# Latent depthwise convolution on TensorE: four-channel block-diagonal matmuls replaced by one 32x64 tile per channel, with its inputs loaded one channel group ahead

## The chip, the cores and the metric

The kernel runs on one core of one Trainium2 chip. The metric is the device time of one execution in microseconds. Before the change the median of three runs is 1877.12 us (1874.78 to 1882.59). Shares and durations below come from one further execution, taken with the hardware profiler.

## The reference, cut to what matters

The reference is one layer of a hybrid backbone: a bidirectional Mamba-2 scan beside a Conformer convolution branch, for 256 context tokens and 2048 latent tokens of width 1024. All data are fp32. The changed part is the convolution branch of the latent tokens, which lie on a grid of 32 rows and 64 columns:

```python
h = ga * jax.nn.sigmoid(gb)                    # (1, 32, 64, 1024)
h = depthwise_conv(h, conv_w, conv_b)          # 31 taps along the 32 rows, each channel by itself
h = layer_norm(h, ln_g, ln_b)                  # over the channels of a token
return jax.nn.silu(h)
```

With 31 taps and 32 rows nearly every output row of a channel depends on every input row. For one channel the convolution is therefore a product of a 32x32 matrix, made of the taps, with the 32x64 grid.

## The kernel before, in words

The tokens are worked on in two halves. In each half the normalised input (`hh`, `hl`: a high and a low part, 128 x 512 pieces) is multiplied with 44 tiles of 128 columns of `w_in`, three passes each (L378, L379, L380 in `mm_cm`). For a tile pair (`gab_unit`, L528) the results `gb` and `ga` become the convolution's input, written to a DRAM tensor `GL[j]` for channel group `j` of 128 channels (L540). `silu_unit` (L542) makes the gates in the same way. These projections are the main stream of the second half, called `blocks`.

Beside this stream run two side streams: the scan (`pass_a`, L648: decay matrices on ScalarE, small matmuls `px`, `py`, `po`, `pst`) and `extra`, which holds the convolutions: for each pair of channel groups `lat_conv`, `ctx_conv` (31 taps on VectorE, L590), `lat_conv`. Python generators give the order: `interleave` (L849) takes one step of `blocks` and then as many side steps as their share, and `merge` (L49) mixes scan and `extra` by their numbers of steps. The framework's scheduler then moves instructions by its own simulated times, so that the order on an engine is not exactly the order of the code. All DMAs of the core are issued in order by SyncE (SP); an issue that waits holds up those behind it.

`lat_conv` (L603) handles one channel group in these steps:

- It loads the bias `cbb`, the taps `kd` (partition = 32 * channel within a group of four + row, 32 rows x 32 groups of four) and the grid `cx` (same partitions, 32 groups x 64 columns). `kd` and `cx` have one buffer each, so that the loads of a channel group wait until the one before has been worked off.
- `expand(u)` (L618) copies the taps of eight groups of four channels into a block-diagonal 128x128 matrix each, in `kbuf`, which was zeroed once (L931). That is four ScalarE copies of 32 x 256 per `u` (L622), sixteen per channel group. There are two `kbuf` buffers.
- For each `u` of four, eight matmuls (L634) multiply the grid of four channels (stationary, 128 rows x 64 columns) with the block-diagonal matrix (moving, 128 columns). Two halves of the channel group go to the two halves of the array's columns (`h`). All matmuls of one `u` fill one PSUM bank of the pool `ss`, which has five banks and is shared with the scan.
- VectorE adds the bias and writes the bank to `cvv` (L639); after the fourth, two DMAs write `cvv` to `CVL` (L644).

A matmul with fp32 operands appears in the profile as two records, each with its own weight load, and one with operands split beforehand (fp32r: L378 to L380, L1078) as one. The eight matmuls of one `u` are thus sixteen records; the eight channel groups make 512 records in 32 groups.

After the blocks and side streams comes the output projection (L1078) with the scan's backward pass and the layer norm that reads `CVL`.

Of the kernel before, what the change touches and what calls it, by code (L numbers as in the profile page):

```python
# [8 lines left out]
F32 = mybir.dt.float32  # L9
# [4 lines left out]
MUL, ADD, SUB, MAX, MIN = ALU.mult, ALU.add, ALU.subtract, ALU.max, ALU.min  # L14
# [3 lines left out]
P = 128  # L18
# [49 lines left out]
def backbone_kernel(ctx, tc, xa, xt_in, cols, rows, wconv, conf_b, gp_row, bg_row, state0, w_mod, w_dt, w_in, w_out,  # L68
                    y_ctx, y_lat, new_state):
    nc = tc.nc  # L70
    V, S, G, T, DMA = nc.vector, nc.scalar, nc.gpsimd, nc.tensor, nc.sync
# [5 lines left out]
    def bank(tag, name):  # L77
        return psp.tile([P, 512], F32, tag=tag, name=name, bufs=3 if tag == "mm" else 5)

    def dram(name, shape):  # L80
        return drp.tile(shape, F32, tag=name, name=name)
# [4 lines left out]
    GL = [dram(f"gl{j}", [P, NT * P]) for j in range(KT)]  # L86
# [87 lines left out]
    cp = ph_c.enter_context(tc.tile_pool(name="cp", bufs=1, side="right"))  # L174

    def ev(name):
        return evp.tile([P, 512], F32, tag="ev", name=name, bufs=3)
# [162 lines left out]
    def load_w(half, c0):  # L340
        t = WCOL.index(c0)
        wl = wp.tile([P, KT, P], F32R, tag="wl", name=f"wl{c0}_{half}", bufs=3)
        wh = wp.tile([P, KT, P], F32R, tag="wh", name=f"wh{c0}_{half}", bufs=3)
        flat = lambda w: w.bitcast(F32).rearrange("p k n -> p (k n)")
        if half:
            DMA.dma_start(flat(wh), WHD[t])
            DMA.dma_start(flat(wl), WLD[t])
            return wh, wl
        for u in range(2):
            ks = slice(4 * u, 4 * u + 4)  # L350
            wr = wp.tile([P, 4, P], F32, tag="wr", name=f"wr{c0}_{u}", bufs=2)
            DMA.dma_start(wr.rearrange("p k n -> p (k n)"), w_in[t * P:(t + 1) * P, u * 512:(u + 1) * 512])
            S.copy(wh[:, ks, :], wr)  # L353
            V.tensor_tensor(wl[:, ks, :], wr, wh[:, ks, :].bitcast(F32), SUB)
        DMA.dma_start(WHD[t], flat(wh))
        DMA.dma_start(WLD[t], flat(wl))
        return wh, wl
# [10 lines left out]
    def next_w():  # L368
        while len(wq) < 3 and wcols:
            wq.append(load_w(*wcols.pop(0)))  # L370
        return wq.pop(0)

    def mm_cm(ps, w, h):
        wh, wl = w
        hh, hl = h
        BN = hh.shape[2]
        for k in range(KT):
            T.matmul(ps[:, :BN], wh[:, k, :], hh[:, k, :], start=(k == 0), stop=False)  # L378
            T.matmul(ps[:, :BN], wh[:, k, :], hl[:, k, :], start=False, stop=False)  # L379
            T.matmul(ps[:, :BN], wl[:, k, :], hh[:, k, :], start=False, stop=(k == KT - 1))  # L380
            yield
# [101 lines left out]
    def xbc_phase(half, first, hb, prep, tails, dtp):  # L483
# [41 lines left out]
        for _ in dtp:  # L525
            pass

    def gab_unit(half, j, hb):  # L528
        wb = next_w()
        wa = next_w()  # L530
        for b in ORDER[half]:
            BN, o = BNS[b], TOK[b]
            pg = bank("mm", f"gb{half}_{j}_{b}")
            yield from mm_cm(pg, wb, hb[b])
            th = ev(f"gth{half}_{j}_{b}")[:, :BN]
            S.activation(th, pg[:, :BN], AF.Tanh, scale=0.5)  # L536
            pa_ = bank("mm", f"ga{half}_{j}_{b}")
            yield from mm_cm(pa_, wa, hb[b])
            V.scalar_tensor_tensor(th, th, 1.0, pa_[:, :BN], ADD, MUL)  # L539
            DMA.dma_start(GL[j][:, o:o + BN], th)  # L540

    def silu_unit(half, c0, dst, j, hb, order=None):  # L542
        w = next_w()
        for b in order or ORDER[half]:
            BN, o = BNS[b], TOK[b] - half * HT[0] * P
            ps = bank("mm", f"sp{half}_{c0}_{j}_{b}")
            yield from mm_cm(ps, w, hb[b])
            th = ev(f"sth{half}_{c0}_{j}_{b}")[:, :BN]
            S.activation(th, ps[:, :BN], AF.Tanh, scale=0.5)  # L549
            V.scalar_tensor_tensor(th, th, 1.0, ps[:, :BN], ADD, MUL)  # L550
            DMA.dma_start(dst[half][j * P:(j + 1) * P, o:o + BN], th)
# [28 lines left out]
    def ctx_conv(j, tile):  # L580
        g = tile(f"cg{j}")
        G.memset(g[:, 0:15], 0.0)
        G.memset(g[:, 271:286], 0.0)
        DMA.dma_start(g[:, 15:271], GL[j][:, 0:256])
        yield
        acc = g[:, 512:768]
        w0 = C_CONFW + j * CW
        V.tensor_scalar(acc, g[:, 0:256], cv[:, w0:w0 + 1], cfb2[:, j:j + 1], MUL, ADD)
        for t in range(1, CW):
            V.scalar_tensor_tensor(acc, g[:, t:t + 256], cv[:, w0 + t:w0 + t + 1], acc, MUL, ADD)  # L590
            if t % 3 == 0:
                yield
        ps = bank("ss", f"cps{j}")
        for t in range(2):
            T.transpose(ps[:, t * P:(t + 1) * P], acc[:, t * P:(t + 1) * P], ident)
        o = g[:, 768:1024]
        S.mul(o, ps[:, :256], 0.5)
        DMA.dma_start(CVC[:, j * P:(j + 1) * P].rearrange("(t p) c -> p t c", p=P),
                      o.rearrange("p (t c) -> p t c", c=P))
        yield  # L600


    def lat_conv(j, lp, kbuf):  # L603
        cbb = lp.tile([P, HD], F32, tag="cbb", name=f"cbb{j}", bufs=2)
        for h in range(2):
            c0 = j * P + h * 64
            DMA.dma_start(cbb[h * 64:(h + 1) * 64], conf_b[c0:c0 + 64].partition_broadcast(64))
        kd = lp.tile([P, 32, 32], F32, tag="kd", name=f"kd{j}", bufs=1)
        for c4 in range(4):
            src = bass.AP(tensor=wconv.tensor, offset=(j * 4 + c4) * 64 * 32, ap=[[32, 32], [1, 1024]])  # L610
            DMA.dma_start(kd[c4 * 32:(c4 + 1) * 32].rearrange("p r g -> p (r g)"), src)

        x = lp.tile([P, 32, 64], F32, tag="cx", name=f"cx{j}", bufs=1)
        src = GL[j][:, 256:].rearrange("(g c) (r w) -> c r g w", c=4, w=64)
        for c4 in range(4):
            DMA.dma_start(x[c4 * 32:(c4 + 1) * 32], src[c4])

        def expand(u):  # L618
            kt = kbuf[u % 2]
            for c4 in range(4):  # L620
                rs = slice(c4 * 32, (c4 + 1) * 32)
                S.copy(kt[rs, :, rs].rearrange("p (h q) r -> p h q r", h=2),  # L622
                       kd[rs].rearrange("p r (h u q) -> p u h q r", h=2, u=4)[:, u])

        vt = lp.tile([P, 32, HD], F32, tag="cvv", name=f"cvv{j}", bufs=1)
        yield
        expand(0)
        yield
        for u in range(4):
            kt = kbuf[u % 2]  # L630
            ps = bank("ss", f"cp{j}_{u}")
            for q in range(4):
                for h in range(2):
                    T.matmul(ps[h * 64:(h + 1) * 64, q * P:(q + 1) * P], x[:, h * 16 + u * 4 + q, :], kt[:, h * 4 + q, :],  # L634
                             start=True, stop=True)
            if u < 3:
                expand(u + 1)
            yield
            V.scalar_tensor_tensor(vt[:, ::-1, u * 16:(u + 1) * 16].rearrange("p r c -> p c r"),  # L639
                                   ps.rearrange("p (c r) -> p c r", r=32), 0.5,  # L640
                                   cbb[:, u * 16:(u + 1) * 16].unsqueeze(2).to_broadcast([P, 16, 32]), MUL, ADD)
        for h in range(2):
            c0 = j * P + h * 64
            DMA.dma_start(CVL[:, c0:c0 + 64].rearrange("(r w) c -> w r c", w=64), vt[h * 64:(h + 1) * 64])  # L644
        yield


    def pass_a(i):  # L648
# [213 lines left out]
    def chain(gens):  # L862
        for g in gens:
            yield from g
# [5 lines left out]
    def post(half, nb):  # L870
        return chain([gab_unit(half, j, hb) for j in range(8)] + [silu_unit(half, Z0, ZS, j, hb) for j in range(8)]
                     + [silu_unit(half, GS0, GS, j, hb) for j in range(nb)])
# [33 lines left out]
    extra = chain([gate_rows()] + [ctx_conv(j, big) for j in range(4)])  # L906
# [19 lines left out]
    ph_b[0].close()  # L926
    ph_l = ExitStack()
    lp = ph_l.enter_context(tc.tile_pool(name="lp", bufs=1, side="right"))
    kbuf = [lp.tile([P, 8, P], F32, name=f"kbuf{u}") for u in range(2)]
    for u in range(2):  # L930
        G.memset(kbuf[u], 0.0)  # L931
    blocks = post(1, 5)
    cg = lambda name: lp.tile([P, D], F32, tag="cg", name=name, bufs=2)
    extra = chain(f for j in range(4) for f in (lat_conv(2 * j, lp, kbuf), ctx_conv(j + 4, cg), lat_conv(2 * j + 1, lp, kbuf)))
    sc_ = scan(range(9, NT))
    run(take(blocks, 24))
    interleave(take(blocks, 24), [sc_] * 4, 24)
# [292 lines left out]
```

## Time and profile before

| what | value |
|---|---|
| median of three runs | 1877.12 us (1874.78 to 1882.59) |
| profiled execution | 1882.2 us, its span 1880.5 us |
| TensorE (PE) busy | 1825.6 us, 97% |
| weight loads (PEld) busy | 1504.6 us, 80% |
| VectorE (DVE) busy | 1188.2 us, 63% |
| ScalarE (ACT) busy | 839.5 us, 45% |
| GpSimd (POOL) busy | 269.0 us, 14% |
| mean DMA rate | 200 GB/s |
| mean granted TensorE clock | 0.986 |
| latent convolution's first and last matmul | 957.8 us and 1336.9 us after the start |

How to read it: a row of the groups gives line, engine, operation, output and inputs by the program's names, sizes and count; then the busy time, the mean time of one in ns, and the idle time of the engine just before, with what ended it. In the timeline the first two columns are start and duration in us, and equal instructions that follow each other are merged into one row. In the waits the columns are the total in us, how often, and the longest. The end of a matmul is modelled, so that the step from one start to the next says more than the duration. PEclk is the share of the full TensorE clock that was granted.

### The profile page before, as it was taken

The page shows a single profiled execution, that of the slowest core. Times are in us where ns is not written, and L with a number is a line of the kernel's source. Part 1 is how long each engine was busy: PE and PEld are TensorE (multiplying, and loading weights), DVE is VectorE, ACT ScalarE, POOL GpSimd, SP SyncE. Part 2 cuts the span into 40 slices and gives each one's busy share as a digit, 9 for nine tenths or more (in the row PEclk, how much of TensorE's full clock was granted, in tenths as well). Part 3 has the DMA queues.
Part 4 walks back from the last instruction along what each step waited for, and adds up shares of the span by engine and source line. Part 5 has one row for each costly group of instructions (what it writes and reads, how often), then busy time and mean ns, then how long its engine had stood idle before and what let it go on. Part 6 is the DMA issues. An engine that isn't in the chain of part 4 may idle for free.

```text
span 1880.5 us, 26833 instructions
## 1 busy us (share of the span) xinstructions
PE 1825.6 (97%) x9739; PEld 1504.6 (80%) x9739; DVE 1188.2 (63%) x1699; ACT 839.5 (45%) x1786; POOL 269.0 (14%) x351
## 2 busy tenths in 40 slices
PE   7899999999999999999999899999999999999998
PEld 4788887787887888888877677777887888888887
DVE  2477887776545553577585768655427676766662
ACT  3646424443455441644355666675414232232321
POOL 0002001111111100100001011110013333333220
PEclk9899999999999999999999999999999999999999
DMA  8556575564677754545587897978887655555532
GB/s 302 212 200 198 211 239 179 176 222 155 211 269 225 225 200 169 165 154 188 179 195 215 210 242 194 278 185 234 239 268 239 191 174 173 165 172 173 175 102 78
DMA packets 290400, 375.29 MB, mean 200 GB/s; under 512 B 85206, under 2 KB 187478, under 8 KB 290268
## 3 DMA queue, kind: packets, MB, share of 16 engines
q1 hardware_dynamic: 290268, 373.58, 64.2%
q8 instruction: 77, 1.26, 0.3%
q14 instruction: 55, 0.45, 0.1%
HBM read 243.92 MB, written 129.59 MB: 199 GB/s over the span
## 4 chain that ended last, share of the span: by engine, by line
PE 62%; DMA 5%; ACT 3%; issue 3%; DVE 2%; SPq 2%; POOL 0%; POOLq 0%; DVEq 0%; ACTq 0%
PE op L1078 20%; PE sp L378 6%; PE sp L379 6%; PE sp L380 6%; DMA lb<-lt 3%; PE xp L379 2%; PE xp L378 2%; PE xp L380 2%; PE py L720 2%; PE ga L378 2%; PE ga L380 1%; PE po L727 1%; PE ga L379 1%; PE qo L985 1%; PE gb L378 1%
## 5 line engine op out<-in xcount | busy, mean ns | idle before, releaser
L684 ACT ACTIVATE lb<-lb,WB 128x128 f32<-128x128 f32 x576 | 184.1, 391 | 150.9 <-POOL lb L676 149.0
L378 PE MATMUL sp<-hh,wh 128*128 128x512 f32 (+1 forms) x640 | 239.7, 375 | 2.6 <-DVE sth L550 2.6
L379 PE MATMUL sp<-hl,wh 128*128 128x512 f32 (+1 forms) x640 | 237.0, 370 | 0.0
L380 PE MATMUL sp<-hh,wl 128*128 128x512 f32 (+1 forms) x640 | 236.7, 370 | 0.2 <-DMA wl<-wld 0.2
L676 POOL TENSOR_SCALAR_AFFINE_SELECT lb<-lb 128x512 f32<-128x512 f32 x144 | 108.7, 760 | 749.7 <-ACT el L673 416.1
L378 PE MATMUL xp<-hh,wh 128*128 128x512 f32 (+1 forms) x480 | 179.1, 375 | 6.1 <-ACT wh L353 4.0
L379 PE MATMUL xp<-hl,wh 128*128 128x512 f32 (+1 forms) x480 | 179.1, 373 | 0.2 <-DVE hl L299 0.2
L380 PE MATMUL xp<-hh,wl 128*128 128x512 f32 (+1 forms) x480 | 179.2, 374 | 0.0
L475 DVE SCALAR_TENSOR_TENSOR cva<-raw,cwh,cva 128x1280 f32<-128x1280 f32 (+1 forms) x96 | 142.7, 1495 | 15.5 <-ACT cva L469 13.6
L378 PEld LDWEIGHTS sp<-hh,wh 128*128 128x128 f32 x640 | 121.0, 189 | 24.3 <-DVE sth L550 3.1
L380 PEld LDWEIGHTS sp<-hh,wl 128*128 128x128 f32 x640 | 121.0, 189 | 21.6 <-DMA wl<-wld 0.7
L379 PEld LDWEIGHTS sp<-hl,wh 128*128 128x128 f32 x640 | 121.2, 189 | 20.1 <-issue 0.5
L378 PE MATMUL gb<-hh,wh 128*128 128x512 f32 (+1 forms) x320 | 121.9, 381 | 3.4 <-DVE gth L539 3.4
L378 PE MATMUL ga<-hh,wh 128*128 128x512 f32 (+1 forms) x320 | 120.4, 376 | 2.6 <-ACT gth L536 2.6
L379 PE MATMUL gb<-hl,wh 128*128 128x512 f32 (+1 forms) x320 | 119.3, 373 | 0.0
L380 PE MATMUL gb<-hh,wl 128*128 128x512 f32 (+1 forms) x320 | 119.1, 372 | 0.0
L380 PE MATMUL ga<-hh,wl 128*128 128x512 f32 (+1 forms) x320 | 118.1, 369 | 0.0
L379 PE MATMUL ga<-hl,wh 128*128 128x512 f32 (+1 forms) x320 | 117.9, 369 | 0.0
L590 DVE SCALAR_TENSOR_TENSOR cg<-cg,cv 128x256 f32<-128x256 f32 x240 | 113.3, 497 | 2.5
L550 DVE SCALAR_TENSOR_TENSOR sth<-sth,sp 128x512 f32<-128x512 f32 (+1 forms) x80 | 50.4, 630 | 98.4 <-ACT sth L549 98.4
L378 PEld LDWEIGHTS xp<-hh,wh 128*128 128x128 f32 x480 | 92.0, 192 | 23.0 <-ACT wh L353 4.8
L688 DVE TENSOR_TENSOR lb<-lb,lb 128x512 f32<-128x512 f32 x72 | 51.6, 717 | 85.6 <-ACT lb L684 55.8
(219 smaller groups left out, 3860.8 us busy)
## 6 DMA issues: line engine op xcount, KB each, us to landing
lb<-lt SPq DMA_DIRECT2D x144, 256.0 KB, 4.2
wr<-in_w_in SPq DMA_DIRECT2D x88, 256.0 KB, 4.9
whd<-wh SPq DMA_DIRECT2D x44, 512.0 KB, 3.4
wld<-wl SPq DMA_DIRECT2D x44, 512.0 KB, 4.7
wh<-whd SPq DMA_DIRECT2D x44, 512.0 KB, 5.2
wl<-wld SPq DMA_DIRECT2D x44, 512.0 KB, 5.6
xT<-xb SPq DMA_DIRECT2D x18, 512.0 KB, 5.4
yp<-yg SPq DMA_DIRECT2D x36, 256.0 KB, 4.5
```

The costliest lines, as they stand in the source:

```text
L378: T.matmul(ps[:, :BN], wh[:, k, :], hh[:, k, :], start=(k == 0), stop=False)
L379: T.matmul(ps[:, :BN], wh[:, k, :], hl[:, k, :], start=False, stop=False)
L380: T.matmul(ps[:, :BN], wl[:, k, :], hh[:, k, :], start=False, stop=(k == KT - 1))
L475: V.scalar_tensor_tensor(a[:, :n], raw[:, t:t + n], cwh[:, ct * 5 + t:ct * 5 + t + 1], a[:, :n], MUL, ADD)
L550: V.scalar_tensor_tensor(th, th, 1.0, ps[:, :BN], ADD, MUL)
L590: V.scalar_tensor_tensor(acc, g[:, t:t + 256], cv[:, w0 + t:w0 + t + 1], acc, MUL, ADD)
L676: G.affine_select(E[g, hq, d], E[g, hq, d], pattern=[[0, 4], [sg, P]], compare_op=ALU.is_ge, fill=NEG, base=0, channel_multiplier=-sg)
L684: S.activation(lb[:, h, :], lb[:, h, :], AF.Exp, bias=WB[:, i, c + h:c + h + 1])
L688: V.tensor_tensor(a, a, E[g, hq, 1], ADD)
L720: T.matmul(py[g][j * HD:(j + 1) * HD, q * P:(q + 1) * P], xt[g][:, h * HD:(h + 1) * HD], E[g, hq, 0][:, t, :], start=True, stop=True)
L727: T.matmul(po[g][:, q * P:(q + 1) * P], Sf[g][:, q * P:(q + 1) * P], bc[:, 2 + g, :], start=True, stop=True)
L1078: T.matmul(pso[n], lhs[:, k % 8, :], w[:, n * 512:(n + 1) * 512], start=(k == 0 and m == 0), stop=(k == 15 and m == 2))
```

## The change

Each channel gets matmuls of its own, on a quarter of the array's rows and half of its columns. The grid stays the stationary operand, now 32 rows x 64 columns, and the moving operand is the 32x32 matrix of that channel. Two channels of a group of four (`a`) and two halves of the channel group (`h`) follow each other in turn, so that four consecutive matmuls use four different tiles of the array and two PSUM banks. A channel group has two groups of 64 matmuls in place of four groups of eight. No block-diagonal matrix is needed: one ScalarE copy per channel group reverses the taps' rows (`kt`). `kd` and `cx` have two buffers, and `lat_load(j + 1)` is called right after the copy of group `j`, if the projections of that group have been issued (`gl_done`); otherwise the group loads its input itself when its turn comes. VectorE's instructions keep their number and size, and write every fourth channel where they wrote sixteen in a row. `lat_conv` has six steps in place of seven.

```diff
+        if half:
+            gl_done.add(j)
...
+    lat_in = {}
+
+    def lat_load(j, lp):
+        kd = lp.tile([P, 32, 32], F32, tag="kd", name=f"kd{j}", bufs=2)
+        x = lp.tile([P, 32, 64], F32, tag="cx", name=f"cx{j}", bufs=2)
         cbb = lp.tile([P, HD], F32, tag="cbb", name=f"cbb{j}", bufs=2)
+        lat_in[j] = kd, x, cbb
...
-        def expand(u):
-            kt = kbuf[u % 2]
-            for c4 in range(4):
-                rs = slice(c4 * 32, (c4 + 1) * 32)
-                S.copy(kt[rs, :, rs].rearrange("p (h q) r -> p h q r", h=2),
-                       kd[rs].rearrange("p r (h u q) -> p u h q r", h=2, u=4)[:, u])
+    def lat_conv(j, lp, more):
+        if j not in lat_in:
+            lat_load(j, lp)
+        kd, x, cbb = lat_in.pop(j)
+        yield
+        kt = lp.tile([P, 32, 32], F32, tag="kt", name=f"kt{j}", bufs=1)
+        S.copy(kt[:, :, ::-1].rearrange("p g r -> p r g"), kd)
+        if more(j + 1):
+            lat_load(j + 1, lp)
+        yield
...
-                    T.matmul(ps[h * 64:(h + 1) * 64, q * P:(q + 1) * P], x[:, h * 16 + u * 4 + q, :], kt[:, h * 4 + q, :],
-                             start=True, stop=True)
-            if u < 3:
-                expand(u + 1)
+                    for a in ps:
+                        rs = slice(a * 32, (a + 1) * 32)
+                        T.matmul(ps[a][h * 64:(h + 1) * 64, q * 32:(q + 1) * 32], x[rs, h * 16 + q, :], kt[rs, h * 16 + q, :],
+                                 start=True, stop=True)
             yield
-            V.scalar_tensor_tensor(vt[:, ::-1, u * 16:(u + 1) * 16].rearrange("p r c -> p c r"),
-                                   ps.rearrange("p (c r) -> p c r", r=32), 0.5,
-                                   cbb[:, u * 16:(u + 1) * 16].unsqueeze(2).to_broadcast([P, 16, 32]), MUL, ADD)
+            for a in ps:
+                V.scalar_tensor_tensor(vt[:, :, a::4].rearrange("p r c -> p c r"),
+                                       ps[a].rearrange("p (c r) -> p c r", r=32), 0.5,
+                                       cbb[:, a::4].unsqueeze(2).to_broadcast([P, 16, 32]), MUL, ADD)
+            yield
...
-    kbuf = [lp.tile([P, 8, P], F32, name=f"kbuf{u}") for u in range(2)]
-    for u in range(2):
-        G.memset(kbuf[u], 0.0)
```

What this does to the order on the engines shows at three places. The first is TensorE in the first channel group; before, a group of the convolution is one row of eight matmuls among the projection's (`ga` is a projection's bank, `cp` one of the convolution's):

```order
L378 MATMUL ga_1_4_8687<-hh_7343,wh_1_8346 128x512
L379 MATMUL ga_1_4_8687<-hl_7344,wh_1_8346 128x512
L380 MATMUL ga_1_4_8687<-hh_7343,wl_1_8345 128x512
L634 MATMUL cp_2_8767<-kbuf_8337,cx_8634 64x128 x8
L378 MATMUL ga_1_4_8687<-hh_7343,wh_1_8346 128x512
```

After, at the same place, 64 small matmuls stand between the projection's, in turn for two banks:

```order
L378 MATMUL ga_1_4_8680<-hh_7343,wh_1_8342 128x512
L379 MATMUL ga_1_4_8680<-hl_7344,wh_1_8342 128x512
L380 MATMUL ga_1_4_8680<-hh_7343,wl_1_8341 128x512
L644 MATMUL cp_0_8685<-kt_8641,cx_8623 64x32
L644 MATMUL cp_1_8686<-kt_8641,cx_8623 64x32
```

The number of groups on TensorE halves, from 32 to 16, and each has eight times as many matmuls, with a quarter of the columns each.

The second place is ScalarE at the second channel group (`kd_9287` are its taps); before, copies into the block-diagonal matrices fill the queue between the scan's work (`xwh`, `lb`) and the projection's (`gth`):

```order
L700 COPY xt_9452<-px_9376 128x512
L622 COPY kbuf_8337<-kd_9287 32x8x32 x4
L710 CAST xwh_9514<-xw_9513 128x512
L622 COPY kbuf_8338<-kd_9287 32x8x32 x4
L684 ACTIVATE lb_9933<-lb_9933,WB 128x128 x4
L622 COPY kbuf_8337<-kd_9612 32x8x32 x3
L622 COPY kbuf_8338<-kd_9612 32x8x32 x2
```

After, one copy (here that of the third channel group) stands there:

```order
L539 ACTIVATE gth_3_4_9548<-gb_3_4_9368 128x512
L709 COPY xt_9648<-px_9531 128x512
L633 COPY kt_9737<-kd_9377 128x32x32
L539 ACTIVATE gth_4_3_9755<-gb_4_3_9685 128x512
L719 CAST xwh_9776<-xw_9775 128x512
```

Of sixteen copies per channel group one is left, and the projection's `gth` no longer stands behind several of them.

The third place is SyncE's queue around the end of the first channel group (`cvl` is the store of its result, `cx` the grid of the second). Before:

```order
L664 DMA lb_9262<-lt_117 128x512
L616 DMA cx_9292<-gl_69 32x32x64 x4
L764 DMA yp_89<-yg_8614 128x512
L644 DMA cvl<-cvv_8639 64x32x64 x2
L664 DMA lb_8997<-lt_117 128x512
```

After, the bias and taps of channel groups that come later (`cbb_9379`, `kd_9739`) are issued there too:

```order
L654 DMA cvl<-cvv_8684 64x32x64
L673 DMA lb_9012<-lt_117 128x512
L619 DMA cbb_9379<-in_conf_b 64x64 x2
L773 DMA yp_89<-yg_8610 128x512
L759 DMA st_107<-sb_8953 128x512
L623 DMA kd_9739<-in_wconv 32x1024 x4
L625 DMA cx_9354<-gl_69 32x32x64 x2
```

The taps of a group now stand in the queue a whole channel group ahead of their use; the number of DMAs is the same.

More of the change, by code (lines that the diff above doesn't have):

```diff
@@ L526, in xbc_phase @@
             pass
+    gl_done = set()
     def gab_unit(half, j, hb):
@@ L530, in gab_unit @@
         wa = next_w()
+        gl_done.discard(j)
         for b in ORDER[half]:
@@ L600, in ctx_conv @@
         yield
-    def lat_conv(j, lp, kbuf):
+    lat_in = {}
+    def lat_load(j, lp):
+        kd = lp.tile([P, 32, 32], F32, tag="kd", name=f"kd{j}", bufs=2)
+        x = lp.tile([P, 32, 64], F32, tag="cx", name=f"cx{j}", bufs=2)
         cbb = lp.tile([P, HD], F32, tag="cbb", name=f"cbb{j}", bufs=2)
+        lat_in[j] = kd, x, cbb
         for h in range(2):
@@ L607, in lat_conv @@
             DMA.dma_start(cbb[h * 64:(h + 1) * 64], conf_b[c0:c0 + 64].partition_broadcast(64))
-        kd = lp.tile([P, 32, 32], F32, tag="kd", name=f"kd{j}", bufs=1)
-        for c4 in range(4):
[L610 to L614, printed above, removed]
@@ L615, in lat_conv @@
-        for c4 in range(4):
-            DMA.dma_start(x[c4 * 32:(c4 + 1) * 32], src[c4])
-        def expand(u):
-            kt = kbuf[u % 2]
-            for c4 in range(4):
-                rs = slice(c4 * 32, (c4 + 1) * 32)
-                S.copy(kt[rs, :, rs].rearrange("p (h q) r -> p h q r", h=2),
-                       kd[rs].rearrange("p r (h u q) -> p u h q r", h=2, u=4)[:, u])
-        vt = lp.tile([P, 32, HD], F32, tag="cvv", name=f"cvv{j}", bufs=1)
-        yield
-        expand(0)
@@ L628, in lat_conv @@
[L628 to L632, printed above, removed]
+        src = GL[j][:, 256:].rearrange("(g a) (r w) -> a r g w", a=4, w=64)
+        for a in range(4):
+            rs = slice(a * 32, (a + 1) * 32)
+            DMA.dma_start(kd[rs].rearrange("p r g -> p (r g)"),
+                          bass.AP(tensor=wconv.tensor, offset=(j * 4 + a) * 64 * 32, ap=[[32, 32], [1, 1024]]))
+            DMA.dma_start(x[rs], src[a])
@@ new lines, in lat_conv @@
+    def lat_conv(j, lp, more):
[8 more added lines that the diff above has]
+        yield
+        vt = lp.tile([P, 32, HD], F32, tag="cvv", name=f"cvv{j}", bufs=1)
+        for a2 in (0, 2):
+            ps = {a: bank("ss", f"cp{j}_{a}") for a in (a2, a2 + 1)}
+            for q in range(16):
@@ L633, in lat_conv @@
                 for h in range(2):
-                    T.matmul(ps[h * 64:(h + 1) * 64, q * P:(q + 1) * P], x[:, h * 16 + u * 4 + q, :], kt[:, h * 4 + q, :],
-                             start=True, stop=True)
-            if u < 3:
-                expand(u + 1)
+                    for a in ps:
+                        rs = slice(a * 32, (a + 1) * 32)
+                        T.matmul(ps[a][h * 64:(h + 1) * 64, q * 32:(q + 1) * 32], x[rs, h * 16 + q, :], kt[rs, h * 16 + q, :],
+                                 start=True, stop=True)
@@ L644, in lat_conv @@
             DMA.dma_start(CVL[:, c0:c0 + 64].rearrange("(r w) c -> w r c", w=64), vt[h * 64:(h + 1) * 64])
-        yield
     def pass_a(i):
@@ L928, in backbone_kernel @@
     lp = ph_l.enter_context(tc.tile_pool(name="lp", bufs=1, side="right"))
-    kbuf = [lp.tile([P, 8, P], F32, name=f"kbuf{u}") for u in range(2)]
-    for u in range(2):
-        G.memset(kbuf[u], 0.0)
     blocks = post(1, 5)
     cg = lambda name: lp.tile([P, D], F32, tag="cg", name=name, bufs=2)
-    extra = chain(f for j in range(4) for f in (lat_conv(2 * j, lp, kbuf), ctx_conv(j + 4, cg), lat_conv(2 * j + 1, lp, kbuf)))
+    lat = lambda j: lat_conv(j, lp, gl_done.__contains__)
+    extra = chain(f for j in range(4) for f in (lat(2 * j), ctx_conv(j + 4, cg), lat(2 * j + 1)))
     sc_ = scan(range(9, NT))
```

## The prediction

> **What bounds the kernel now.** I read the page, then the waits of TensorE in the stage of the latent convolution (900 to 1350 us), then the timeline around one of its groups. The page:
>
> ```profile
> span 1880.5 us, 26833 instructions
> PE 1825.6 (97%) x9739; PEld 1504.6 (80%) x9739; DVE 1188.2 (63%) x1699; ACT 839.5 (45%) x1786; POOL 269.0 (14%) x351
> ```
>
> TensorE is the path nearly everywhere, so an edit is worth what it does to TensorE's own time and waits. What TensorE waited for in the stage (total in us, times, longest):
>
> ```profile
> PE cp L634 <- ACT kbuf L622: 10.0, 6, 2.7
> PE pb L771 <- DVE yo L741: 2.1, 1, 2.1
> PE px L696 <- issue: 2.0, 2, 1.6
> PE cp L634 <- DMA cx<-gl: 1.9, 1, 1.9
> ...
> PE cp L634 <- DVE cvv L639: 0.3, 1, 0.3
> ```
>
> Most of it is the convolution's matmuls `cp` waiting: 10.0 + 1.9 + 0.3 = 12.2 us. The largest wait, with the copies on ScalarE that it waited for:
>
> ```profile
> 1037.58 0.39 PE L380 MATMUL gb<-hh,wl 128*128 128x512 f32 x1
> 1040.64 1.25 PE L634 MATMUL cp<-kbuf,cx 128*64 128x128 f32 x10 [2.67 <-ACT kbuf L622]
> ```
> ```profile
> 1037.97 2.62 ACT L622 COPY kbuf<-kd 32x256 f32<-32x256 f32 x4
> ```
>
> ScalarE reached the four copies at 1037.97, behind the scan's work, and TensorE stood until they ended. After three such stalls the granted clock (the number after POOL) was low:
>
> ```profile
> 1036.00:1046.00 10.00, 7.33 (x37) 5.62 (x35) 10.00 (x18) 8.94 (x19) 0.78 (x1) 0.83 0.39 116
> 1172.00:1184.00 12.00, 7.97 (x58) 6.72 (x57) 6.03 (x8) 10.87 (x25) 1.90 (x3) 0.72 0.84 248
> 1255.00:1265.00 10.00, 8.09 (x49) 5.96 (x49) 3.98 (x7) 6.76 (x17) 0.63 (x1) 0.83 1.17 209
> ```
>
> That is 0.17 x 10 + 0.28 x 12 + 0.17 x 10 = 6.8 us of clock lost, which I charge to the stalls.
>
> **What the convolution costs now.** A group undisturbed, and sixteen records of the scan's `qo`, with as many moving columns but on the full array:
>
> ```profile
> 957.53 0.39 PE L380 MATMUL ga<-hh,wl 128*128 128x512 f32 x1
> 957.85 1.09 PE L634 MATMUL cp<-kbuf,cx 128*64 128x128 f32 x16
> 958.87 0.50 PE L378 MATMUL ga<-hh,wh 128*128 128x512 f32 x1
> 959.21 0.40 PE L379 MATMUL ga<-hl,wh 128*128 128x512 f32 x1
> 959.44 0.39 PE L380 MATMUL ga<-hh,wl 128*128 128x512 f32 x1
> ...
> 1434.29 2.03 PE L985 MATMUL qo<-ct,Sb 128*128 128x128 f32 x16
> 1436.08 0.71 PE L1078 MATMUL op<-woh,pl 128*128 128x512 f32 x2
> ```
>
> From 957.53 to 959.21 are 1.68 us; two projection matmuls in it take 0.23 each (959.21 to 959.44). The group costs 1.22 us, and 32 groups 39.0 us. With waits and clock the convolution holds TensorE for 39.0 + 12.2 + 6.8 = 58.0 us.
>
> The inside of a group gives the rate. `qo` steps by (1436.08 - 1434.29)/16 = 0.112 us a record. `cp` steps by (958.87 - 957.85)/16 = 0.064, so its two column halves run side by side, as eight rounds of two records.
>
> **The change: TensorE.** 1024 matmuls of 32x64 stationary and 32 moving columns make 2048 records, 128 in each of 16 groups. Their duration isn't in the trace; it is worked out from records of other widths (ns: shortest, median, longest):
>
> ```profile
> L634 PEld LDWEIGHTS cp<-kbuf,cx x512: 132/137/231, 957.8 to 1336.8; 128*64 128x64 f32 x171
> L634 PE MATMUL cp<-kbuf,cx x512: 272/273/476, 957.8 to 1336.9; 128*64 128x128 f32 x171
> ```
> ```profile
> L239 PEld LDWEIGHTS mp<-wm,sc x128: 81/85/129, 13.6 to 34.6; 128*2 128x2 f32 x128
> L239 PE MATMUL mp<-wm,sc x128: 378/379/634, 13.6 to 34.9; 128*2 128x256 f32 x128
> ```
>
> A weight column costs (137 - 85)/62 = 0.84 ns, so 64 take 54 ns. A moving column costs (379 - 273)/128 = 0.83 ns, so 128 take 106 ns and 32 take 27. The next load runs under the current matmul: `qo`'s 112 ns are one load of 128 columns (107) and 5 of step, not load plus matmul. So a round of `cp` is 106 + 5 = 111 ns today, what a group costs beyond its rounds is 1.22 - 8 x 0.111 = 0.33 us, and a tile of the new form turns a record in 54 + 5 = 59 ns, bound by the weight load.
>
> What no row shows is whether the two row halves of the array run side by side as the column halves do. If all four tiles do, a group is 32 rounds: 32 x 0.059 + 0.33 = 2.22 us, and 16 groups take 35.5 us. If only two do, 64 rounds: 4.11 us, 65.7 us in all. If none does: 7.88 us and 126 us. I take four: the column halves overlap without loss, the row halves read other partitions and write another PSUM bank, and the code takes the four tiles in turn. The nearest row is `cp` itself.
>
> Can the sequencer deliver eight instructions (four loads, four matmuls) per round of 59 ns? After a stall at 1065 us it shows its pace:
>
> ```profile
> L634 PEld LDWEIGHTS cp<-kbuf,cx x16: 133/137/137, 1065.5 to 1066.3; 128*64 128x64 f32 x16
> L720 PEldq EVENT_SEMAPHORE  x1: 51/51/51, 1065.6 to 1065.6; - x1
> ```
>
> The semaphore instruction of L720 stands behind these 16 loads and 16 matmuls; it was reached at 1065.6, when the first load was 0.1 us old. 32 instructions in at most 0.2 us are 6 ns each, against 7 needed. It suffices, narrowly.
>
> **The change: waits.** Sixteen copies per channel group become one:
>
> ```profile
> L622 ACT COPY kbuf<-kd 32x256 f32<-32x256 f32 x128 | 83.3, 657 | 19.6 <-DMA kd<-in_wconv 11.8 <-PE cp L634 6.0
> L1019 ACT CAST yh<-y 128x1024 fp32r<-128x1024 f32 x18 | 19.0, 1053 | 24.8 <-DVE y L1013 23.9
> ```
>
> The new copy has 1024 elements per partition: between 1.05 us (the contiguous cast) and 4 x 0.657 = 2.6 us (as strided as today). I take 2.6, since it is strided too. That is the length of one of today's four `expand` steps, so TensorE is exposed to ScalarE once per channel group, not four times. I keep a quarter of waits and clock, (12.2 + 6.8)/4 = 4.8 us; bounds are 0 and all 19.0.
>
> Sum: 35.5 + 4.8 - 58.0 = -17.7 us. The profiled execution's own 1882.2 becomes 1864.5; it lies 5.1 above the median of 1877.1, which becomes **1859**.
>
> **The rest, at nothing.** ScalarE loses 83.3 us and gains 8 x 2.6; off the path except for the wait counted. VectorE's 32 instructions stay, at
>
> ```profile
> L639 DVE SCALAR_TENSOR_TENSOR cvv<-cp,cbb 128x512 f32<-128x512 f32 x32 | 33.9, 1064 | 6.5 <-PE cp L634 5.9 <-DMA cvl<-cvv 0.5
> ```
>
> Two now follow each group, 2.1 us, before the banks are free; the scan shares these five banks, and what stands behind is its next matmul. Projections hide it (the order has 21 or more matmuls between the two groups, about 5 us at 0.23). Without that cover it would cost up to 16 x 1.1 us. On SyncE's queue the loads come earlier, so a stall goes:
>
> ```profile
> SPq L611 <- ACT kbuf L622: 24.1, 7, 7.5
> ```
>
> Here the queue stood still for a free `kd` buffer, with the scan's `lb` loads behind it. TensorE waits for no DMA but `cx` (1.9 us, counted), so that is worth nothing more; without two buffers it would come back. The last channel group's steps now end inside the blocks; its groups lay among projections before, so this too is nothing.
>
> **The rivals.**
>
> *Only two tiles at a time* (0.18). 65.7 + 4.8 - 58.0 = +12.5 us: 1890, or 1885 without any wait. For it: nothing in the trace runs row halves together. Against it: the columns do. [...]
>
> *Slower: loads one after another* (0.10). If a weight load of one row half holds up the other's and the column halves' too, 128 records take 0.059 each: 126 + 4.8 - 58.0 = +73 us, 1950. It decides from a round of ((58.0 - 4.8)/16 - 0.33)/32 = 0.094 us on: above that the convolution costs more than today.
>
> *Slower: the sequencer* (0.02). At today's 0.064 a record, were that its limit and not the array's, 2048 records would take 131, and 131 + 16 x 0.33 + 4.8 - 58.0 = +83 us: 1960. The row of L720 above speaks against it: 16 loads and 16 matmuls in 0.2 us. [...]
>
> *The clock falls in the groups* (0.08). For 2 us at a time the array streams only 27 of 59 ns. If each group costs a lapse like that at 1036 us, 1.7 us, it is 16 x 1.7 = 27.2: -17.7 + 27.2 = +9.5, 1887. For it: clocks fell near stalls of 2 us. Against: those were full stops.
>
> *ScalarE is late all the same* (0.07). If all 19.0 us stay, 35.5 + 19.0 - 58.0 = -3.5: 1874, which a measurement can't tell from no change.
>
> **How the numbers follow.** The forecast has 0.55. Its own range is -22.5 (no wait left) to -9.4, 1855 to 1868. A measurement of this kernel tells 0.5% or 9.4 us from no change. Faster by more: 0.55. Within: 0.07 for the late ScalarE, 0.09 of the pairs, 0.05 of the clock, 0.21 in all. Slower: 0.09 and 0.03 of those two, 0.12 for the slower rivals, 0.24. The range must reach the pairs at 1890 and the clock at 1887; with some 5 us below the forecast's own end for the small terms taken at nothing I give 1850 to 1892, which leaves out the 0.12 and little else.
>
> **What would show it.** Right: a group of `cp` of about 2.2 us between projections, four records per 0.059 us; waits of `cp` on ScalarE under 6 us; granted clock near 1.0 at 1000 to 1300 us; ScalarE's copies near 21 us. Wrong: groups of 4 us (pairs) or over 7 us (one by one, or the sequencer, in which case loads start evenly spaced); a clock under 0.9 in undisturbed groups; waits of `cp` on banks held by VectorE or the scan.

## The result, and the profile after

The changed kernel takes 1948.62 us (median of 4 runs, 1945.81 to 1952.65), the kernel before 1879.86 us beside it. The ratio is 1.0369 (95% interval 1.0335 to 1.0403): 68.8 us slower, where 18 us faster was forecast. The profiled execution of the changed kernel took 1948.61 us. Its page begins:

```profile
span 1946.5 us, 29765 instructions
PE 1841.1 (95%) x11275; PEld 1519.6 (78%) x11275; DVE 1189.6 (61%) x1699; ACT 774.0 (40%) x1666; POOL 267.9 (14%) x349
```

TensorE is busy 15.5 us longer than before, in a span that is 66 us longer; the rest is idle time. First the part that was forecast: a group of the convolution in the timeline of TensorE.

```profile
952.49 0.39 PE L380 MATMUL ga<-hh,wl 128*128 128x512 f32 x1
952.80 2.07 PE L644 MATMUL cp<-kt,cx 32*64 32x32 f32 x128
954.80 0.50 PE L378 MATMUL ga<-hh,wh 128*128 128x512 f32 x1
955.14 0.40 PE L379 MATMUL ga<-hl,wh 128*128 128x512 f32 x1
```

From 952.49 to 955.14 are 2.65 us, less two projection matmuls of 0.23: the group costs 2.19 us. The 16 groups are 35.0 us of work at full clock, against 39.0 before. Ten of the sixteen ran like this one, in 2.07 us without a break; the others were interrupted by a wait or ran at a lower clock. The copies on ScalarE, by tile:

```profile
L633 ACT COPY kt<-kd x8: 2039/2082/2149, 936.6 to 1324.7; 128x1024 f32<-128x1024 f32 x8
```

Eight copies of 2.08 us are 16.7 us, where 83.3 stood before, and TensorE never waits for one. What it waits for now (stretch 950 to 1420 us):

```profile
PE cp L644 <- DVE cvv L648: 22.1, 6, 11.5
PE px L705 <- DVE cvv L648: 17.6, 2, 12.8
PE ga L378 <- DMA wh<-whd: 10.8, 2, 9.3
PE pst L742 <- DVE cvv L648: 6.0, 1, 6.0
PE cp L644 <- DVE yg L770: 3.5, 1, 3.5
```

The first, second and fourth row are one thing: a matmul (of the convolution, or of the scan) needs a bank that VectorE has not yet emptied into `cvv`; 45.7 us. Before, that row had 0.3. The third row is a projection waiting for its weights; the longer of its two waits ended with a load that SyncE issued at 1111.84, behind a store of `cvv` and loads of the next channel group. With VectorE's order, below, 0.9 us of the 10.8 are left. The windows of the same stretch, of the kernel before and of the changed one (after the stretch and its length: busy time of TensorE, its weight loads, VectorE, ScalarE, GpSimd; granted clock, busy share of the DMA engines, GB/s):

```profile
950.00:1420.00 470.00, 452.31 (x2603) 357.85 (x2602) 289.85 (x461) 258.61 (x571) 48.23 (x70) 0.98 0.83 226
```
```profile
950.00:1420.00 470.00, 398.21 (x3814) 316.68 (x3813) 263.48 (x428) 179.77 (x436) 43.19 (x64) 0.92 0.71 187
```

TensorE's idle time went from 17.7 to 71.8 us, and the clock from 0.98 to 0.92. The two profiled spans differ by 66.0 us. Idle time is 54.1 of it in this stretch (outside it there is 3.6 us less), and busy time 15.5: -4.0 for the groups' work, and 19.5 that are left, most of it for the lower clock. Added up over the trace's record of the clock, TensorE's busy time lost 24.9 us to it in this stretch (busy time times the share that was not granted), and 7.7 before.

Why VectorE is late shows in its own timeline, at the first group, whose matmuls were through at 954.8:

```profile
952.64 9.19 DVE L595 SCALAR_TENSOR_TENSOR cg<-cg,cv 128x256 f32<-128x256 f32 x23
961.76 1.86 DVE L648 SCALAR_TENSOR_TENSOR cvv<-cp,cbb 128x512 f32<-128x512 f32 x2
```

The two steps themselves take 1.9 us. But they stand in the queue behind 23 taps of context convolutions, so that the banks come free 8.8 us after the last matmul. The largest wait of this kind inside a group, on all engines in order of time (`kd` and other DMAs left out):

```profile
1071.49 0.30 PE L644 MATMUL cp<-kt,cx 32*64 32x32 f32 x2
...
1073.16 0.42 SPq L673 DMA_DIRECT2D lb<-lt  x1
1077.58 3.14 SPq L625 DMA_DIRECT2D cx<-gl  x4
1078.66 0.84 ACT L682 ACTIVATE el<-lb 64x256 f32<-64x256 f32 x2 [19.56 <-DMA lb<-lt]
1079.57 0.64 POOL L685 TENSOR_SCALAR_AFFINE_SELECT lb<-lb 128x512 f32<-128x512 f32 x1 [29.56 <-ACT el L682]
1080.24 1.28 ACT L693 ACTIVATE lb<-lb,WB 128x128 f32<-128x128 f32 x4 [0.74 <-POOL lb L685]
1081.61 0.69 DVE L697 TENSOR_TENSOR lb<-lb,lb 128x512 f32<-128x512 f32 x1 [14.58 <-ACT lb L693]
1082.21 1.89 DVE L648 SCALAR_TENSOR_TENSOR cvv<-cp,cbb 128x512 f32<-128x512 f32 x2
...
1083.28 1.50 PE L644 MATMUL cp<-kt,cx 32*64 32x32 f32 x48 [11.49 <-DVE cvv L648]
```

Read from below: TensorE waits for a bank that VectorE is to empty into `cvv`, a bank of the group before, whose matmuls started at 1060.67 us; that step stands behind the scan's `lb`, before which VectorE stood idle 14.58 us; `lb` waits for ScalarE, GpSimd, ScalarE again, and in the end for a load that SyncE issued at 1073.16. The bank's matmuls were through when the next projection started at 1063.74 us, and the store of the old `cvv`, issued from 1061.46 on, landed 8.2 us after its issue. Yet VectorE, idle until 1081.61, did not take the step ahead of `lb`: it ran it at 1082.21, right behind. So the scan's lateness becomes the convolution's.

It goes the other way too. SyncE's queue had stood still for 15.3 us ahead of that load (1046 to 1074 us):

```profile
SPq L623 <- ACT kt L633: 8.3, 1, 8.3
SPq L654 <- DVE cg L595: 7.0, 1, 7.0
```

The first row is a load of taps that waits for ScalarE's copy `kt`. The second is the store of the channel group before (L654). It was issued at 1061.46, when VectorE's last two steps into `cvv` had ended (1061.44; the row names a tap that stands beside them), themselves behind 13 taps. A late `cvv` thus delays the scan's `lb`, and a late `lb` the next `cvv`. The clock after that stall:

```profile
1083.00:1093.00 10.00, 9.72 (x155) 8.17 (x155) 4.21 (x7) 4.16 (x12) 1.76 (x2) 0.63 0.66 160
```

Ten microseconds of matmuls at 0.63 cost 3.7 us on top of the 11.5.

### The profile page after: what moved, and what is told of

It is laid out like the page before. It is cut to its first block, busy times and chain, and to the rows that moved or that the text cites. A ratio compares the mean times of both kernels' runs of the same rounds, so it can differ in the third digit from the quotient of the medians.

```text
span 1946.5 us, 29765 instructions
## 1 busy us (share of the span) xinstructions
PE 1841.1 (95%) x11275; PEld 1519.6 (78%) x11275; DVE 1189.6 (61%) x1699; ACT 774.0 (40%) x1666; POOL 267.9 (14%) x349
## 5 line engine op out<-in xcount | busy, mean ns | idle before, releaser
L378 PE MATMUL ga<-hh,wh 128*128 128x512 f32 (+1 forms) x320 | 123.6, 386 | 13.0 <-DMA wh<-whd 10.8
L682 ACT ACTIVATE el<-lb 64x256 f32<-64x256 f32 x136 | 56.4, 415 | 166.7 <-DMA lb<-lt 148.8
```

The costliest lines, as they stand in the source:

```text
L682: S.activation(el[g][rs, q:q + 2, :], E[g, hq, 0][rs, j::2, :], AF.Exp)
```

## The experiments

Three theories were set against each other. *Loads*: the early loads stand in SyncE's queue ahead of the scan's and make the scan late. *Pairs*: two banks per group, of five shared with the scan, are too many. *Order*: on the other engines' queues the reader that frees a bank stands behind other work, long or not ready, because the order suits a TensorE that is slower than this one now is. (*Pairs* is called 'banks' in the first expectations.) All times are medians; each is compared with the kernel before on the same chip. Idle time and clock are those of one profiled execution each.

| run | us | ratio to before (95%) | TensorE idle, 950 to 1420 us | clock there |
|---|---|---|---|---|
| changed kernel | 1948.62 | 1.0369 (1.0335 to 1.0403) | 71.8 | 0.92 |
| loads at own turn | 1948.37 | 1.036 (1.0332 to 1.0388) | 69.3 | 0.91 |
| before, loads ahead | 1889.48 | 1.0045 (1.0026 to 1.0064) | 26.2 | 0.98 |
| one bank | 1924.2 | 1.0233 (1.0206 to 1.0259) | 23.5 | 0.97 |
| emptied by ScalarE | 1942.91 | 1.0337 (1.0306 to 1.0368) | 61.6 | 0.92 |
| row halves in turn | 1958.65 | 1.0422 (1.0397 to 1.0446) | 32.9 | 0.89 |
| six banks | 1987.46 | 1.057 (1.0542 to 1.0599) | 77.9 | 0.90 |
| VectorE's order | 1897.22 | 1.009 (1.0062 to 1.0119) | 34.8 | 0.96 |
| half groups | 1916.54 | 1.0206 (1.0174 to 1.0239) | 38.3 | 0.95 |
| both orders | 1879.72 | 0.9999 (0.9983 to 1.0014) | 17.0 | 0.97 |
| VectorE's order, own turn | 1898.73 | 1.0093 (1.0065 to 1.012) | 32.7 | 0.96 |
| before, VectorE's order | 1880.88 | 0.9998 (0.9984 to 1.0013) | 23.6 | 0.97 |
| both orders, half groups | 1875.21 | 0.9964 (0.9952 to 0.9977) | 13.0 | 0.98 |

### Is it the loads?

Loads at their own turn:

```diff
-    lat = lambda j: lat_conv(j, lp, gl_done.__contains__)
+    lat = lambda j: lat_conv(j, lp, lambda n: False)
```

> The changed kernel, but each channel group loads its bias, taps and grid when its own turn comes (two buffers each stay, the matmuls, the banks and VectorE's steps stay). Theory 'loads' (the early loads stand in SyncE's queue ahead of the scan's lb loads and wait there for taps' buffers and for stores; the scan is late, VectorE's queue stands behind it, and the convolution's banks are freed late): most of TensorE's 72 us of waits in the stage go, 1870 to 1890 us. Theory 'banks' (two of five banks per group, freed only behind VectorE's other work): nothing of that depends on when the loads are issued, 1935 to 1960 us, waits of cp and px on cvv stay near 48 us.

1948.37 us, and TensorE's waits are the same ones:

```profile
PE cp L644 <- DVE cvv L648: 21.3, 6, 10.0
PE px L705 <- DVE cvv L648: 16.2, 2, 11.8
```

The opposite, the old matmuls with the loads ahead:

```diff
+            if u == 2 and more(j + 1):
+                lat_load(j + 1, lp)
...
-        kd = lp.tile([P, 32, 32], F32, tag="kd", name=f"kd{j}", bufs=1)
+        kd = lp.tile([P, 32, 32], F32, tag="kd", name=f"kd{j}", bufs=2)
```

(and `cx` alike.)

> The kernel before with one part of the change alone: taps and grid with two buffers, the next group's loads issued after the third of the four groups of matmuls. Matmuls, copies and bank use stay as before. Theory 'loads': the queue of SyncE stands still as in the changed kernel, 1915 to 1950 us. Theory 'banks': no harm, 1870 to 1885 us (TensorE's 1.9 us of waits on cx and SyncE's 24 us on the taps' buffer go).

1889.48 us, between the two, 4.5 us above the range of "no harm" and 26 below that of the loads. Loading ahead costs some 9 us with the old matmuls. With the new ones it costs nothing that shows, neither here nor in the last pair of runs below. Theory *loads* falls as the cause.

### Is it the pairs of banks?

One channel of four at a time, one bank per group:

```diff
-        for a2 in (0, 2):
-            ps = {a: bank("ss", f"cp{j}_{a}") for a in (a2, a2 + 1)}
+        for a1 in range(4):
+            ps = {a: bank("ss", f"cp{j}_{a}") for a in (a1,)}
...
-            yield
```

> The changed kernel with one channel of four at a time: one bank per group of 32 matmuls, its VectorE step behind it, as many groups (32) and steps per group as before the change; loads ahead as changed. Only the two column halves can run side by side, so TensorE's own work rises: 32 groups of (16 rounds x 2 records x 0.059 + 0.33) = 2.2 us, 71 us in place of 35.5. Theory 'banks': waits on cvv fall under 10 us, and the time is 1948 - 48 - most of the 30 us of lost clock + 35, about 1895 to 1915 us. Theory 'loads': the waits stay and the matmuls are added, 1970 to 1990 us.

1924.2 us: in neither range, but TensorE's waits on `cvv` are down to 4.1 and 1.7 us, and `cp` has none:

```profile
PE px L704 <- issue: 5.9, 2, 3.6
PE pst L741 <- DVE yo L749: 4.8, 1, 4.8
PE px L704 <- DVE cvv L648: 4.1, 2, 2.2
...
PE pst L741 <- DVE cvv L648: 1.7, 1, 1.7
```

It pays 35 us more of matmuls and is still 24 faster than the changed kernel. That fits *pairs*, and it fits *order* too, since TensorE is slower here. Two runs part them. The first keeps the pairs and makes TensorE slower; the second keeps TensorE fast and gives it a bank more.

```diff
-            for q in range(16):
-                for h in range(2):
-                    for a in ps:
-                        rs = slice(a * 32, (a + 1) * 32)
+            for a in ps:
+                rs = slice(a * 32, (a + 1) * 32)
+                for q in range(16):
+                    for h in range(2):
```

> The changed kernel with the loop over the two channels of a pair outside: the same 64 matmuls into the same two banks, but one row half after the other, so that only column halves run side by side. A group takes 2 x 1.84 + 0.33 = 4.0 us on TensorE in place of 2.2 (from the one-bank run's 1.84 us per 32 matmuls), 16 x 1.8 = 29 us more work; the order on all engines stays nearly as in the changed kernel. Theory 'pairs' (two of five banks per group are too many): the waits stay, 1970 to 1985 us. Theory 'order' (the order on VectorE, ScalarE and SyncE was laid out for a TensorE that stays longer in a group than it does; it runs ahead and then stands still for them): TensorE arrives later, the waits shrink by about what was added, and the time stays at 1935 to 1955 us.

1958.65 us. A group that nothing disturbed takes 3.72 us in place of 2.07:

```profile
1192.17 3.72 PE L644 MATMUL cp<-kt,cx 32*64 32x32 f32 x128
```

So 26 us of work were added, and 10 came out. Idle time fell by 38.9 us, from 71.8 to 32.9, and the waits of `cp` on `cvv` from 22.1 to 8.8; but busy time lost 47.1 us to the clock in place of 24.9 (more on that at the end). It is nearer to *order* than to *pairs*, though 4 us outside its range: what idleness gave back, the clock took in part.

```diff
-    bufs=3 if tag == "mm" else 5
+    bufs=2 if tag == "mm" else 6
```

> The changed kernel with six banks for the scan and the convolution, and two in place of three for the projections. Theory 'pairs': waits of cp, px and pst on cvv fall from 47 us to under 15, 1890 to 1915 us (some us go to the projections' two banks). Theory 'order': VectorE's work in front of the two steps stays, one bank more shifts the stall by one matmul of the scan, 1935 to 1965 us.

1987.46 us, slower than either expected:

```profile
PE ga L378 <- DVE gth L542: 34.1, 5, 13.9
PE cp L644 <- DVE cvv L648: 15.0, 4, 8.1
PE gb L378 <- ACT gth L539: 14.8, 3, 8.1
```

The sixth bank lowers the waits of `cp` on `cvv` from 22.1 us to 15.0, and those of `px` drop out of the list, which would fit pairs that press on the five. But TensorE now stands still for the projections' banks as well, so that it comes later to everything else, and this alone would shorten those waits. The bank taken from the projections costs more than the sixth gives: they wait for their readers `gth`, on VectorE and ScalarE. It doesn't decide between the theories.

### Is it VectorE, or the queue?

ScalarE empties the banks (the bias is left out):

```diff
-                V.scalar_tensor_tensor(vt[:, :, a::4].rearrange("p r c -> p c r"),
-                                       ps[a].rearrange("p (c r) -> p c r", r=32), 0.5,
-                                       cbb[:, a::4].unsqueeze(2).to_broadcast([P, 16, 32]), MUL, ADD)
+                S.mul(vt[:, :, a::4].rearrange("p r c -> p c r"), ps[a].rearrange("p (c r) -> p c r", r=32), 0.5)
```

> The changed kernel with the banks emptied by ScalarE (times 0.5) in place of VectorE; the bias of the convolution is left out. Bank pairs and loads ahead stay. If the banks are late because VectorE's in-order queue stands behind the context convolution and the scan: waits on cvv fall from 48 us to under 15, 1880 to 1905 us. Theory 'loads': ScalarE's queue stands behind the scan's lb loads just as VectorE's does, the waits change their name and the time stays at 1930 to 1955 us.

1942.91 us. ScalarE had been busy for only 179.77 of 470 us in the changed kernel's row above, and yet:

```profile
PE px L703 <- ACT cvv L648: 17.1, 2, 9.5
PE cp L644 <- ACT cvv L648: 14.2, 4, 7.8
```

The wait changes its name. So it isn't that VectorE has too much to do: on ScalarE's queue, which carries the scan as well, the same steps come late too. My range for the wait on VectorE failed, and the one given to *loads* came, for a reason that is *order*'s.

### Changing nothing but the order

VectorE's two steps right behind their matmuls in the code, and what the code issues later on VectorE kept behind them (an order of issue without a wait):

```diff
-            yield
+            behind()
             for a in ps:
-                V.scalar_tensor_tensor(vt[:, :, a::4].rearrange("p r c -> p c r"),
+                st = V.scalar_tensor_tensor(vt[:, :, a::4].rearrange("p r c -> p c r"),
...
+            behind(st)
             yield
+            yield
```

`behind(st)` opens `tc.issue_after(st.ins)`, which holds for VectorE until the next `behind()`.

> The changed kernel; VectorE's two steps are issued right behind a group's matmuls in the code, and what the code issues on VectorE later stays behind them in its queue (an order of issue, no wait). Context convolutions of later channel groups can then no longer stand in front. Same work, same banks, same loads. Theory 'order': waits on cvv fall from 47 us to under 12, lost clock to about 10 us, 1870 to 1895 us. Theory 'pairs': the banks are short all the same, 1925 to 1955 us.

1897.22 us: 51 us come back, with the same work, banks and loads. That is 2 us above the range of *order* and 28 below that of *pairs*. By the traces, the time from a group's last matmul to the end of its two steps was a median of 10.3 us in the changed kernel (at most 20.3); now it is 2.1. Waits on `cvv` are gone from the list, and SyncE's `lb` loads wait 15.3 us for VectorE's `lb` in place of 83.0 (35.5 before the change). What leads TensorE's list now is

```profile
PE po L746 <- ACT sb L768: 12.6, 1, 12.6
PE cp L652 <- ACT sb L768: 9.4, 2, 6.5
```

`sb` is the copy that frees the scan's state bank, on ScalarE, where it stands behind `lb` work that isn't ready; at the longest wait:

```profile
1070.75 0.40 ACT L703 ACTIVATE lb<-lb,WB 128x128 f32<-128x128 f32 x1 [7.14 <-POOL lb L695]
...
1073.30 0.57 ACT L768 COPY sb<-pst 128x512 f32<-128x512 f32 x1
```

It is the same mechanism on the next queue. So the same cure there, for the scan's steps of this stage:

```diff
-            S.copy(sb, pst[g, 1])
+            if i >= 9:
+                behind(on="S")
+            st = S.copy(sb, pst[g, 1])
+            if i >= 9:
+                behind(st, "S")
```

> The run with VectorE's order, and the same done on ScalarE: each copy of the scan's state (sb, the reader that frees the scan's state bank pst) keeps its place in the code, and what the code issues later on ScalarE stays behind it. Theory 'order': the 22 us of waits of po and cp on sb (ScalarE's copy stood behind lb work that waits for its loads) and some 12 us of clock go, 1860 to 1878 us. Theory 'late scan' (the scan's chain of loads, masks and exponentials is itself too slow for the faster TensorE): the waits only change their name, 1888 to 1905 us.

1879.72 us, ratio 0.9999: all of the loss is back, by two orders. It lies 2 us above the range of *order* and well below that of a scan that is too slow in any order. But a piece of the latter is in it:

```profile
PE ga L378 <- ACT xt L720: 6.6, 1, 6.6
PE py L740 <- DVE lb L709: 5.1, 1, 5.1
PE px L716 <- DVE Sf L763: 2.7, 1, 2.7
PE cp L653 <- ACT sb L771: 1.3, 1, 1.3
```

Together with small ones this is 17.0 us of idle time, as much as the 17.7 before the change, when it was the convolution that waited for its copies.

Two controls. First VectorE's order with the loads at their own turn:

```diff
-    lat = lambda j: lat_conv(j, lp, gl_done.__contains__)
+    lat = lambda j: lat_conv(j, lp, lambda n: False)
```

> The run with VectorE's order, but each channel group loads its input when its own turn comes. Theory 'order': no difference as without it, 1890 to 1903 us. Theory 'loads' in a weak form (the early loads cost some us that the stalls hid): 1875 to 1888 us.

1898.73 against 1897.22 us: no difference, so that the loads' cost wasn't hidden behind the waits on `cvv` either (with both orders this was not run). And VectorE's order in the kernel before:

```diff
-            yield
-            V.scalar_tensor_tensor(vt[:, ::-1, u * 16:(u + 1) * 16].rearrange("p r c -> p c r"),
+            behind()
+            st = V.scalar_tensor_tensor(vt[:, ::-1, u * 16:(u + 1) * 16].rearrange("p r c -> p c r"),
...
+            behind(st)
+            yield
```

> The kernel before, with its VectorE step right behind each group's matmuls in the code and what the code issues later on VectorE behind it. It says whether the order helps only the changed kernel. Theory 'order' (the old groups last about as long on TensorE as the order was laid out for, so their banks were free in time: 0.3 us of waits on cvv): 1872 to 1890 us. If this order is better for any of the two kernels: 1840 to 1860 us.

1880.88 us, ratio 0.9998: their order wasn't a reserve. It was not that the old readers came at once. From a group's last matmul to the end of its step it took a median of 4.2 us before the change, and 1.2 in this run; but each old group held one bank of the five, and the 4.2 us cost TensorE 0.3 us of waits.

### Groups in halves

A group of 64 matmuls in two parts with projections between them, alone:

```diff
-            for q in range(16):
+            for q0 in (0, 8):
+                for q in range(q0, q0 + 8):
...
+                yield
```

> The changed kernel with each group of 64 matmuls issued in two parts of 32, with projections between them; still four tiles in turn, two banks and VectorE's two steps at the end. TensorE pays a group's 0.33 us sixteen times more, 5 us. Theory 'order': TensorE leaves VectorE more time between a group's first and last matmul, part of the waits goes, 1905 to 1935 us. Theory 'pairs': the two banks are held longer, 1950 to 1975 us.

1916.54 us: 32 faster than the changed kernel, though the parts cost an estimated 5 us (16 times the prediction's 0.33) and hold the banks longer. TensorE does other work while VectorE comes up to the group. It speaks for *order* and against *pairs*. With both orders as well, the projections stand after the first part only, and VectorE's steps right behind the second:

```diff
-            for q in range(16):
+            for q0 in (0, 8):
+                for q in range(q0, q0 + 8):
...
+                if not q0:
+                    yield
```

> Both orders, and each group of 64 matmuls in two parts with projections between them. Theory 'order': with the queues in order the parts only cost, 16 x 0.33 = 5 us over the run with both orders, 1865 to 1883 us. If TensorE's running ahead costs beyond the queues: below the run with both orders.

1875.21 us, ratio 0.9964 (0.9952 to 0.9977), faster than before the change and 4.5 us faster than whole groups, where I had expected 5 more. The waits are

```profile
PE px L718 <- ACT sb L773: 7.5, 2, 6.6
PE cp L654 <- ACT cb L810: 1.9, 1, 1.9
PE px L718 <- issue: 1.5, 1, 1.5
```

Idle time is 13.0 us. This is the only version of the new matmuls that beats both kernels, by 0.36%.

## Why the prediction was wrong

**What the convolution costs on TensorE: right.** 2.19 us a group where 2.22 was forecast, 35.0 in all where 35.5. Four records start per round of (954.80 - 952.80)/32 = 0.0625 us with the group's tail in it; the forecast had 0.059. All four tiles work side by side, the sequencer keeps up (256 loads and matmuls in 2.00 us, 7.8 ns each), and the rivals of pairs of tiles, of loads one after another and of the sequencer are out. That the measured 1949 us lies on the second one's 1950 is chance: its mechanism needs groups above 7 us. One ground for the four tiles was weaker than the prediction had it. The step of 0.064 us (against 0.112) shows that the matmuls of the two column halves overlap, but not that their weight loads do: two loads of an estimated 0.054 us one after the other fit into a round of two steps, 0.128 us, as well. That the loads of different columns overlap was thus a guess that came true; this result (128 records in 2.00 us) and the one-bank run (64 in 1.98 us) show it.

**ScalarE: right.** No wait for a copy, and 16.7 us of copies (bound 20.8).

**The step that failed is "The rest, at nothing",** in its sentence on VectorE: "Two now follow each group, 2.1 us, before the banks are free ... Projections hide it", with 16 x 1.1 us as the most that it could cost. I took the duration of the two steps for the time until the banks are free. What counts is when they are reached: 23 taps or a 14.58 us wait of the scan stood ahead of them, and the banks came free a median of 10.3 us after a group, not 2.1. The bound was wrong in kind, since it priced the instructions and not the queue. The price was some 46 us of waits on `cvv`, more on the other queues, and the clock. The prediction did name "waits of `cp` on banks held by VectorE or the scan" as a sign that it is wrong, but gave it no rival and no chance, and no price beyond those 17.6 us.

**The kept waits and clock, 4.8 us:** mis-sized for the same reason. Even with both queues in order they came out not at a quarter of the old ones but at the whole: 17.0 us of idle time against 17.7. I asked which of the convolution's waits would go, not what would be late next. While TensorE waited for the copies, the scan's chain had time to get ready; without those waits it is the scan that TensorE waits for (that the one took the other's place is how I read the equal sums; no run shows it by itself). That leaves 4.0 us of work, of which 0.9 shows in the medians (1879.72 against 1880.66). The clock took back some of it (busy time lost 9.1 us to it in the stretch, 7.7 before); the rest is less than executions of one kernel differ by (1875.72 to 1887.28 for the kernel before).

**The loads: right in size, by luck in part.** "Worth nothing more" holds with the new matmuls (0.3 and 1.5 us); with the old ones they cost 9.

**The clock** fell behind the stalls, as in the row of 1083 us (0.63), and not by itself in the ten undisturbed groups (1.00 in each, and in the microsecond behind it), so that this rival's mechanism is out at groups of 2 us.

**What stays open.** Shown is that order alone, on two queues, brings back all of the 69 us, and that the old groups didn't need it. That a slower TensorE needs it less fits the runs with row halves in turn and with one bank. Whether late readers would have cost as much with the fast groups and one bank each was not run, so that the pairs are out as a cause by themselves, but not as a condition. That the scheduler put the readers late because it reckons more time for 64 small matmuls than they take is argued from this; no trace shows what it reckons. That `lat_conv` has six steps in place of seven was not tried alone.

## What to carry to other kernels

When work on the critical engine gets shorter, ask for each buffer that it fills what stands ahead of the reader in the reader's queue, and how long that can wait; the reader's own duration says nothing on it. An engine that is idle half of the time can still be late if its queue is shared with a chain that isn't ready: ScalarE was busy for 210 of 470 us in the run where it emptied the banks, and TensorE waited 31.3 us for those steps. If a change that makes an engine's work shorter moves the time the wrong way, try the order of the freeing instructions first: here the order on two queues was worth 69 us, and the cheaper matmuls 4 us of TensorE's time.

## What the hardware showed besides

Tiles of the array overlap in both directions. Column halves with all rows in common: 64 records of the one-bank run take from 956.53 to 958.51.

```profile
956.53 2.05 PE L644 MATMUL cp<-kt,cx 32*64 32x32 f32 x64
958.51 0.50 PE L378 MATMUL ga<-hh,wh 128*128 128x512 f32 x1
```

That is 1.98 us for 64 records, and 2.00 us for 128 when the row halves take turns as well. In a one-bank group all 64 records use the same 32 rows. Their 64 loads one after the other would take 64 x 0.054 = 3.5 us, an estimate with the prediction's price of a load (from the rows of L634 and L239); the 1.98 us say that the loads of the two column halves overlap too.

The clock also fell without any wait. In the run with row halves in turn TensorE was never idle from 950 to 972 us, and its clock by windows was

```profile
950.00:958.60 8.60, 8.60 (x120) 7.27 (x120) 7.84 (x19) 1.22 (x2) 0.00 (x0) 1.00 1.29 214
958.60:965.40 6.80, 6.80 (x53) 5.77 (x50) 6.80 (x17) 0.00 (x0) 0.00 (x0) 0.50 0.31 125
965.40:972.20 6.80, 6.80 (x125) 5.62 (x126) 6.80 (x17) 0.62 (x1) 0.00 (x0) 1.00 0.13 41
```

In the timeline the group of that run, which would have ended at 959.8 at full clock, is

```profile
956.09 4.65 PE L644 MATMUL cp<-kt,cx 32*64 32x32 f32 x128
```

It and the projections behind it lose 0.50 x 6.8 = 3.4 us. Of the thirteen groups of this run that no wait interrupted, the clock fell in ten, or within a microsecond of their end; in the changed kernel it fell in none of the ten such groups of 2 us. At full clock a group takes 3.72 us in this run and 2.07 in the changed kernel. From which length on the clock falls, and what in a group brings it down, was not shown.
